# Spreading a norm's factors over the partitions: one full-precision product replaced by two rounded products of a high and a low part

## The chip, the cores and the metric

The kernel runs on one core of a Trainium2 chip. The metric is the device time of one execution in microseconds. TensorE (PE in the profile) does the matrix products, VectorE (DVE), ScalarE (ACT) and GpSimd (POOL) the element-wise work, and transfers are issued from SyncE's and ScalarE's queues.

## What is computed

One decoder layer over 2048 positions with 1024 channels, in float32, and a last norm. Cut to what matters:

```python
def rms_norm(x, g):
    y = x * lax.rsqrt(jnp.mean(x * x, axis=-1, keepdims=True) + EPS)
    return y * g

h = rms_norm(x, norm1_g)
proj = h @ w_in                       # 1024 x 2048
a = spatial_gating(proj[..., :1024])  # gelu, layer norm, 128 x 128 mixing
c = conformer_conv(proj[..., 1024:])  # gate, causal conv of width 31, norm, silu
x = x + concat([a, c]) @ w_out
h = rms_norm(x, norm2_g)              # the "second norm"
x = x + square(relu(h @ w_ff1)) @ w_ff2
return rms_norm(x, final_g)           # the "last norm"
```

The norm's factor is one number per position: 1/sqrt(mean of squares + eps).

## The kernel before

Channels lie on the partitions and positions on the free axis. The 2048 positions are worked in four blocks of 512 (blocks 0 to 3); blocks 0 and 1 form pair 0, blocks 2 and 3 form pair 1 of the feed-forward part. All large products are made from float32 operands split into a high part (rounded to fp32r) and a low part (the rest), with three fp32r products in place of one full-precision product (`mm3`). The two feed-forward matrices are multiplied with a seven-product scheme (the numbers 1 to 7 in `ORDER`, `BANK`, `INTO`).

**Stages in order.** For each block the value and gate projections (`stage_v`, `stage_g`) with the convolution as a chain of 31 VectorE steps per channel group that runs in the background; then the output projection (`stage_o`) with the residual. Block 0's `stage_o` stands before block 3's `stage_v`, and block 1's behind block 3's `stage_g`. Then `multiply("u0")` is the first feed-forward matrix for pair 0, `stage_o` of blocks 2 and 3 follow, then `multiply("u1")`, and last sixteen `down_chunk` calls, eight per pair, for the second matrix.

**The factors.** In the second norm the squares of a block are added up on GpSimd; `feature_sums` sums them over the partitions with eight short products (tile `ssum`), so that the sum of a position lies on a partition. VectorE makes `ve` (mean and eps) and GpSimd the power -1/2 (tile `r`, 128 x 4). To multiply by the factor where positions lie on the free axis, the 512 factors must stand in every partition. `spread` (and in the last norm `times_ident`) writes the identity scaled by each of the four columns of `r` to a 128 x 512 tile `dg` on VectorE, and a product with a matrix of ones (tile `rbc`) puts each factor in all partitions. This product is made in full float32, which the trace shows as two MATMUL instructions. The second norm's result is copied by ScalarE to `r_rows`, and used by `up_out` when the first feed-forward product is taken out of its bank. The last norm's result (tile `rbc3` in the program; the profile shows it as `rbc`) is used by eight VectorE multiplications that make the output.

**Who calls it.** `row_scale(b)` is called once for each block 0 to 3 at the end of its `stage_o`. `later(n, f)` runs `f` n beats on: the sums in one beat, `rsqrt` one beat on, `spread_out` two on (it issues the `dg` multiplication), `product` three on (it issues the product), and the copy to `r_rows` four on. A beat is one group of twelve products in `stage_o` and in `multiply`. `finish(b, acc)` does the last norm of blocks 0 and 1 in steps, with the pauses `gaps` between them, while the second half of the `down_chunk` calls runs. Block 3 goes through `finish_third` and block 2 through `finish_last`; the first norm goes through `make_h` and `stage_v`.

**Order of the work.** Each engine works its instructions in the order in which they were issued to it. Blocks marked `tc.manual_schedule()` keep the program's order: `stage_o` of all blocks, both `multiply` calls and the last `down_chunk`. In the others (`stage_v`, `stage_g`, the first fifteen `down_chunk` calls) a list scheduler sets the order on each engine. A planner inside the kernel keeps a clock for each engine, with a cost per instruction (`dve`, `dsb`, `gps`, `pe`, `pe4`), and uses it for two choices: `background` issues convolution steps while VectorE's clock is more than `SLACK` behind TensorE's, and `rest` gives a low part to GpSimd or to VectorE.

Temporary tiles of 128 x 512 (`tmp`) come from a ring of ten, tiny tiles (`small`) from rings of four.

Of the kernel before, what the change touches and what calls it, by code (L numbers as in the profile page):

```python
# [9 lines left out]
F32 = mybir.dt.float32  # L10
F32R = mybir.dt.float32r
BF16 = mybir.dt.bfloat16
AF = mybir.ActivationFunctionType
ALU = mybir.AluOpType

P = 128
# [66 lines left out]
def hybrid_block_kernel(  # L83
# [15 lines left out]
    dve = Clocked(nc.vector, lambda n: 0.35 if n <= 128 else 0.17 + n / 960.0)  # L99
    dcv = Clocked(nc.vector, lambda n: 0.15 + n / 960.0, dve.clock)  # L100
    dsb = Clocked(nc.vector, lambda n: 0.22 + n / 512.0 if n <= 512 else n / 640.0, dve.clock)
    gps = Clocked(nc.gpsimd, lambda n: 0.35 + n / 488.0 if n > 8 else 1.1)
    pe = Clocked(nc.tensor, lambda n: 0.0135 + n / 2400.0)
    pe4 = Clocked(nc.tensor, lambda n: 0.0135 + n / 600.0, pe.clock)

    const = ctx.enter_context(tc.tile_pool(name="const", bufs=1))
    small = ctx.enter_context(tc.tile_pool(name="small", bufs=4))
# [32 lines left out]
    def tmp(name, dtype=F32):  # L140
        return t2.tile([P, 512], dtype, tag="tmp", name=name)
# [4 lines left out]
    def mm_tile(name):  # L146
        return bank("mm", name)

    def tp_tile(name):
        return bank("tp", name)  # L150

    def tiny(name, n=4):
        return small.tile([P, n], F32, tag=f"{name}{n}", name=name)

    def act_pair(name):
        return slot(f"{name}_hi", F32R), slot(f"{name}_lo", F32R)

    def split(src, hi, lo):

        nc.scalar.copy(hi, src)  # L160
        rest(src, hi, lo)
# [13 lines left out]
    def halves(pair):  # L175
        return [(pair[0][:, a * 512:a * 512 + 512], pair[1][:, a * 512:a * 512 + 512])
                for a in range(2)]
# [56 lines left out]
    ident = const.tile([P, P], F32, name="ident")  # L234
    make_identity(nc, ident)
    ones = const.tile([P, P], F32, name="ones")
# [11 lines left out]
    def v(off, j):  # L248
        return vec[:, off + j:off + j + 1]

    def rsqrt(dst, src, mul):
        n = dst.shape[1]
        ve = tiny("ve")
        dve.tensor_scalar(ve[:, :n], src, mul, EPS, op0=ALU.mult, op1=ALU.add)
        gps.tensor_tensor(dst, ve[:, :n], nhalf.to_broadcast([P, n]), op=ALU.pow)
# [148 lines left out]
    def norm1(b, r):  # L404

        ss = tiny("ss")
        xin = []

        def load(i):
            xin.append(slot("xin"))  # L410
            nc.sync.dma_start(xin[i], x[(4 * b + i) * P:(4 * b + i + 1) * P, :])

        load(0)
        for i in range(4):
            if i < 3:
                load(i + 1)
            yield
            junk = t2.tile([P, 1024], BF16, tag="tmp", name="junk")
            nc.scalar.activation(junk, xin[i], AF.Square, accum_out=ss[:, i:i + 1])
        rsqrt(r, ss, 1.0 / D)  # L420

    def spread(r, ps):

        dg = tmp("dg")
        n = r.shape[1]
        dsb.tensor_tensor(
            dg.rearrange("p (n t) -> p n t", t=P)[:, :n, :],
            ident.unsqueeze(1).to_broadcast([P, n, P]),
            r.unsqueeze(2).to_broadcast([P, n, P]), op=ALU.mult)
        yield  # L430
        pe4.matmul(ps, ones, dg[:, :n * P], start=True, stop=True)

    def make_h(b, h):
        r = tiny("r1")
        yield from norm1(b, r)
        yield
        ps = tp_tile("rbc")
        yield from spread(r, ps)
        hf = []

        def load(k):
            hf.append(tmp("hf"))
            nc.sync.dma_start(hf[k], xt[b, k // 2, :, k % 2, :])

        load(0)
        for k in range(KD):
            if k < KD - 1:
                load(k + 1)
            yield
            if k % 2 == 0:  # L450
                pair = halves(act_pair("h"))
            dve.scalar_tensor_tensor(
                hf[k], hf[k], v(V_G1, k), ps, op0=ALU.mult, op1=ALU.mult)
            split(hf[k], *pair[k % 2])
            h.append(pair[k % 2])
# [32 lines left out]
    def feature_sums(acc, n, pc=None):  # L488

        pc = tp_tile("ssum") if pc is None else pc  # L490
        for i in range(n):
            for k, sq in enumerate(acc):
                pe4.matmul(pc[:, i:i + 1], sq[:, i * P:(i + 1) * P], ones[:, 0:1],
                           start=k == 0, stop=k == len(acc) - 1)
        return pc[:, :n]
# [100 lines left out]
    def later(n, f, first=False):  # L596
        due.append([n, f, first])
# [25 lines left out]
    def row_scale(b):  # L623

        r = r2[b]

        def spread_out():
            ps = tp_tile("rbc")
            g = spread(r, ps)
            next(g)  # L630

            def product():
                next(g, 0)
                later(1, lambda: nc.scalar.copy(r_rows[:, b % 2, :], ps))
            later(1, product)

        def sums():
            ps = feature_sums(acc[b], 4)
            later(1, lambda: rsqrt(r, ps, 1.0 / D))
            later(2, spread_out)  # L640
        return sums
# [100 lines left out]
    queue.append(make_cbias())  # L742
    late, rows0 = stage_v(0, h[0], parts[0], r0)
    queue.append(make_h(1, h[1]))
    stage_g(0, h[0], parts[0], late, rows0)
    drain()
    late, _ = stage_v(1, h[1], parts[1])
    queue.append(make_h(2, h[2]))
    slow.append(first_units())
    stage_g(1, h[1], parts[1], late)  # L750
    drain()
    late, _ = stage_v(2, h[2], parts[2])
    queue.append(split_mix(parts[0], mix[0]))
    queue.append(load_resids(0))
    stage_g(2, h[2], parts[2], late)
    drain()
    queue.append(make_h(3, h[3]))
    dve.time += BEHIND
    with tc.manual_schedule():
        stage_o(0, lambda d: tick(1))  # L760
    drain()
    late, _ = stage_v(3, h[3], parts[3])
# [212 lines left out]
    def up_out(pair):  # L975
        kept = {}

        def out(m, i, ps):
            blk_ = INTO[i]
            def copy():  # L980
                kept[m, blk_] = tmp("c")
                nc.scalar.copy(kept[m, blk_], ps)  # L982

            def finish():
                if i == 4:
                    src, c = ps, tmp("c")
                else:
                    c = kept.pop((m, blk_))
                    src = c if i == 7 else ps
                    dve.tensor_tensor(src, ps, c, op=ALU.add)  # L990
                (dsb if i == 7 else dve).scalar_tensor_tensor(
                    c, src, 0.0, r_rows[:, blk_[1], :], op0=ALU.max, op1=ALU.mult)
                later(1, lambda: nc.scalar.activation(c, c, AF.Square))  # L993
                later(2, lambda: nc.scalar.dma_start(
                    f_d[pair][m // 2, 2 * blk_[0] + blk_[1], :, m % 2, :], c))

            later(1, copy if i in (1, 5, 6) else finish, True)
        return out
# [65 lines left out]
    with tc.manual_schedule():  # L1064
        stage_o(2, at_o2)
        pace["w2"] = 0.0
        k = w2st.at[2]
# [58 lines left out]
    def finish(b, acc):  # L1126

        gaps = (6, 3, 4)
        for _ in range(gaps[0]):
            yield  # L1130
        r = tiny("r1")
        ve = tiny("ve")
        ps = feature_sums(acc, 4, mm_tile("ssum"))
        yield
        dve.tensor_scalar(ve, ps, 1.0 / D, EPS, op0=ALU.mult, op1=ALU.add)
        gps.tensor_tensor(r, ve, nhalf.to_broadcast([P, 4]), op=ALU.pow)
        for _ in range(gaps[1]):
            yield
        dg = tmp("dg")
        times_ident(dg, r)  # L1140
        for _ in range(gaps[2]):
            yield
        ps = mm_tile("rbc3")
        pe4.matmul(ps, ones, dg, start=True, stop=True)
        x = dn["x"][b]
        for k in range(KD):
            yield
            dve.scalar_tensor_tensor(x[k], x[k], v(V_FG, k), ps, op0=ALU.mult, op1=ALU.mult)
            nc.sync.dma_start(out[b, k // 2, :, k % 2, :], x[k])

    def times_ident(dg, r):
        dsb.tensor_tensor(
            dg.rearrange("p (n t) -> p n t", t=P), ident.unsqueeze(1).to_broadcast([P, 4, P]),
            r.unsqueeze(2).to_broadcast([P, 4, P]), op=ALU.mult)
# [235 lines left out]
```

## Time and profile before

| | us |
|---|---|
| three runs | 1828.97, 1831.97, 1837.33 |
| median | 1831.97 |
| profiled execution, its time | 1831.89 |
| profiled execution, its span | 1830.2 |

The span runs from the first to the last instruction of the core; 1.7 us of the execution lie around it. A row of the profile gives the engine, the operation, the tile written and the tiles read, the shape and the count, and then the busy time or the duration. L78 is the line of the helper that records nearly every operation, so rows are told apart by their tiles. A row of the timeline begins with the start and the duration in us; in brackets at its end stands how long the engine sat idle before it, and what ended that.

### The profile page before, as it was taken

How to read it: one execution, taken by the hardware profiler on the slowest of the kernel's cores; microseconds unless marked ns; L12 is line 12 of the kernel's file. 1: busy time of each engine (PE TensorE's matmuls, PEld its weight loads, DVE VectorE, ACT ScalarE, POOL GpSimd, SP SyncE). 2: the span in 40 equal slices, each digit the busy share in tenths (PEclk: the TensorE clock that was granted, in tenths of full speed). 3: DMA queues.
4: the chain of work that ended last, by engine and by line, in shares of the span. 5: the costliest groups of instructions: out<-in, count | busy, mean ns of one | idle time of the engine just before them, and what ended most of it. 6: DMA issues, size and time to landing. Idle time of an engine off the chain costs nothing. (4 is left out here: it accounts for less than half of the span.)

```text
span 1830.2 us, 23249 instructions
## 1 busy us (share of the span) xinstructions
PE 1809.3 (99%) x8080; PEld 1488.5 (81%) x8080; DVE 1330.8 (73%) x1825; ACT 758.6 (41%) x1172; POOL 1233.3 (67%) x775
## 2 busy tenths in 40 slices
PE   9999999999999999999999999999999999999998
PEld 6888878888888888888888888888788888888886
DVE  5699997997998985632567787676866568665655
ACT  6345565454445445455354545432322231212112
POOL 4575975883766666699878989776945465444434
PEclk9999999999999999999999999999999999999999
DMA  8342655432645456685557778998987679767652
GB/s 327 112 164 91 229 178 213 184 125 83 220 150 189 161 195 202 215 293 204 208 184 266 270 258 298 355 408 335 412 326 248 252 272 327 299 238 256 254 191 93
DMA packets 131686, 424.74 MB, mean 232 GB/s; under 512 B 14576, under 2 KB 15216, under 8 KB 131568
## 3 DMA queue, kind: packets, MB, share of 16 engines
q1 hardware_dynamic: 96000, 329.12, 50.5%
q10 hardware_dynamic: 35568, 94.13, 13.2%
q8 instruction: 64, 1.05, 0.2%
q14 instruction: 54, 0.44, 0.1%
HBM read 302.60 MB, written 120.59 MB: 231 GB/s over the span
## 5 line engine op out<-in xcount | busy, mean ns | idle before, releaser
L78 PE MATMUL py<-fo_hi,w2o 128*128 128x512 f32 x1792 | 555.9, 391 | 0.8 <-DVE x L78 0.8
L78 POOL TENSOR_TENSOR fo_lo<-fraw,fo_hi 128x1024 fp32r<-128x1024 f32 x111 | 274.4, 2481 | 252.9 <-ACT fo_hi L160 210.7
L78 DVE TENSOR_TENSOR x<-py,x 128x512 f32<-128x512 f32 x448 | 300.9, 687 | 185.8 <-PE py L78 185.4
L78 PEld LDWEIGHTS py<-fo_hi,w2o 128*128 128x128 f32 x1792 | 337.1, 188 | 72.0 <-DVE x L78 1.2
L78 PE MATMUL py<-hop,w1o 128*128 128x512 f32 x1536 | 363.8, 390 | 0.5 <-ACT c L982 0.4
L78 PE MATMUL py<-fo_lo,w2o 128*128 128x512 f32 x896 | 349.7, 390 | 0.9 <-POOL fo_lo L78 0.8
L78 PEld LDWEIGHTS py<-hop,w1o 128*128 128x128 f32 x1536 | 287.6, 188 | 62.4 <-issue 1.4
L78 DVE SCALAR_TENSOR_TENSOR acc<-g,vec,acc 128x512 f32<-128x512 f32 x464 | 322.9, 746 | 1.2
L160 ACT CAST fo_hi<-fraw 128x1024 fp32r<-128x1024 f32 x112 | 117.0, 1052 | 413.7 <-PE py L78 218.0
L78 POOL TENSOR_TENSOR w_lo<-raw,w_hi 128x1024 fp32r<-128x1024 f32 (+1 forms) x94 | 224.1, 2392 | 53.9 <-ACT w_hi L160 39.6
L78 POOL TENSOR_TENSOR w1o<-wraw,w1o 128x512 fp32r<-128x512 f32 x120 | 172.0, 1438 | 55.6 <-ACT w1o L810 43.4
L78 PEld LDWEIGHTS py<-fo_lo,w2o 128*128 128x128 f32 x896 | 168.6, 188 | 37.9 <-POOL fo_lo L78 2.6
L78 PE MATMUL pz<-hop,w1o 128*128 128x512 f32 x768 | 183.8, 390 | 0.0
L78 POOL TENSOR_TENSOR w1o<-ws,w1o 128x512 fp32r<-128x512 f32 x90 | 128.7, 1433 | 66.4 <-ACT w1o L810 62.6
L78 PEld LDWEIGHTS pz<-hop,w1o 128*128 128x128 f32 x768 | 143.8, 188 | 29.8
L78 DVE TENSOR_TENSOR fraw<-fraw 128x1024 f32<-128x1024 f32 x64 | 93.1, 1455 | 13.3 <-POOL fo_lo L78 13.2
L993 ACT ACTIVATE c<-c 128x512 f32<-128x512 f32 x128 | 80.8, 631 | 52.5 <-DVE c L78 52.0
L78 PE MATMUL po<-m_hi,w_hi 128*128 128x512 f32 x256 | 101.1, 395 | 0.0
L78 PE MATMUL po<-m_hi,w_lo 128*128 128x512 f32 x256 | 99.8, 390 | 0.6 <-POOL w_lo L78 0.6
L78 PE MATMUL po<-m_lo,w_hi 128*128 128x512 f32 x256 | 99.7, 389 | 0.0
L78 DVE TENSOR_TENSOR px<-px,c 128x512 f32<-128x512 f32 x32 | 22.3, 698 | 100.9 <-PE px L78 67.8
L78 POOL TENSOR_TENSOR w2p<-wraw,w2p 128x512 fp32r<-128x512 f32 x64 | 93.5, 1463 | 2.6 <-ACT w2p L810 2.6
(155 smaller groups left out, 2947.9 us busy)
## 6 DMA issues: line engine op xcount, KB each, us to landing
w2o<-w_d SPq DMA_DIRECT2D x224, 512.0 KB, 6.0
w_d<-w2p ACTq DMA_DIRECT2D x112, 512.0 KB, 5.4
wraw<-in_w SPq DMA_DIRECT2D x92, 512.0 KB, 4.7
f_d<-c ACTq DMA_DIRECT2D x128, 256.0 KB, 4.1
fraw<-f_d SPq DMA_DIRECT2D x64, 512.0 KB, 6.8
raw<-in_w_ct SPq DMA_DIRECT2D x48, 512.0 KB, 5.0
raw<-in_w_o SPq DMA_DIRECT2D x32, 512.0 KB, 5.4
w1o<-w_d SPq DMA_DIRECT2D x28, 512.0 KB, 5.5
```

What stands on the lines that cost most here:

```text
L78: return op(out, *args, **kwargs)
L160: nc.scalar.copy(hi, src)
L993: later(1, lambda: nc.scalar.activation(c, c, AF.Square))
```

## The change

Two new functions are added, and two callers use them. `r_pair` copies `r` to a tile rounded to fp32r (`rh`), subtracts to get the rest (`rl`), and makes two scaled identities. `r_sum` makes two fp32r products into one bank, the high part and then the low part.

```diff
+    def r_pair(r):
+        n = r.shape[1]
+        rh, rl = [small.tile([P, n], F32R, tag=f"rh{n}", name="rh") for _ in range(2)]
+        dve.tensor_copy(rh, r)
+        dve.tensor_tensor(rl, r, rh.bitcast(F32), op=ALU.subtract)
+        pair = [tmp("dg", F32R) for _ in range(2)]
+        for dg, part in zip(pair, (rh, rl)):
+            dsb.tensor_tensor(
+                dg.rearrange("p (n t) -> p n t", t=P)[:, :n, :],
+                ident.unsqueeze(1).to_broadcast([P, n, P]),
+                part.bitcast(F32).unsqueeze(2).to_broadcast([P, n, P]), op=ALU.mult)
+        return pair
+
+    def r_sum(ps, pair):
+        for k, dg in enumerate(pair):
+            pe.matmul(ps, ones.bitcast(F32R), dg, start=k == 0, stop=k == 1)
...
         def spread_out():
             ps = tp_tile("rbc")
-            g = spread(r, ps)
-            next(g)
+            pair = r_pair(r)
             def product():
-                next(g, 0)
+                r_sum(ps, pair)
                 later(1, lambda: nc.scalar.copy(r_rows[:, b % 2, :], ps))
...
-        dg = tmp("dg")
-        times_ident(dg, r)
+        pair = r_pair(r)
         for _ in range(gaps[2]):
             yield
         ps = mm_tile("rbc3")
-        pe4.matmul(ps, ones, dg, start=True, stop=True)
+        r_sum(ps, pair)
```

The second hunk is in `row_scale` (blocks 0 to 3), the third in `finish` (last norm, blocks 0 and 1). The other spreads keep the full-precision product.

## The prediction

> **What bounds the kernel now.** I read the page's busy times first, then the chain of work that ended last, then the waits of TensorE, and last the timeline of VectorE, GpSimd and TensorE around each of the six spreads that change.
>
> ```profile
> span 1830.2 us, 23249 instructions
> PE 1809.3 (99%) x8080; PEld 1488.5 (81%) x8080; DVE 1330.8 (73%) x1825; ACT 758.6 (41%) x1172; POOL 1233.3 (67%) x775
> ```
>
> TensorE is busy for 1809.3 of 1830.2 us. So any TensorE time that is taken away is gained, and any wait that TensorE gets is lost, wherever it happens. The chain shows what a product costs in the row of products, and so what the change can win:
>
> ```profile
> 1513.68 0.86 PE rbc L78 x2
> 1514.54 18.60 PE py L78 x82
> ...
> 1544.97 0.86 PE rbc L78 x2
> ```
>
> An fp32r product of 128x512 moves the chain on by 18.60/82 = 0.227 us. A full-precision spread (two MATMULs) moves it on by 0.86. Today TensorE hardly ever waits for the scaled identity; this is the only such row among its waits (sum, count, longest):
>
> ```profile
> PE rbc L78 <- DVE dg L78: 0.3, 1, 0.3
> ```
>
> **The gain on TensorE.** Each of the six spreads loses one product of 0.86 and gets two of 0.227: 0.86 - 0.454 = 0.41 us less. Six of them are 2.5 us, 0.14% of the time. That is all there is to win.
>
> **The price on VectorE.** Before the product VectorE does one 128x512 multiplication (`dg`). After the change it does four operations in a row: a copy of 128x4, a subtraction of 128x4 and two multiplications. TensorE takes its instructions in order, so if the second multiplication isn't done when TensorE gets to the second product, everything behind it waits. How long the four take hangs on GpSimd. Block 1 shows it (VectorE's row, then GpSimd's, then TensorE's):
>
> ```profile
> 501.35 1.79 DVE L78 TENSOR_TENSOR dg<-ident,r 128x512 f32<-128x512 f32 x1 [1.13 <-POOL r L78]
> ```
> ```profile
> 501.29 1.30 POOL L78 TENSOR_TENSOR hop<-xr,hop 128x512 fp32r<-128x512 f32 x1
> 502.55 1.75 POOL L78 TENSOR_TENSOR hop<-xr,hop 128x512 fp32r<-128x512 f32 x1
> ...
> 501.29 7.99 POOL L78 TENSOR_TENSOR hop<-xr,hop 128x512 fp32r<-128x512 f32 x6
> ```
> ```profile
> 505.22 1.02 PE L78 MATMUL rbc<-dg,ones 128*128 128x512 f32 x2
> ```
>
> GpSimd begins its next work 0.06 us before `dg` can start. `dg` ends 0.6 us after the GpSimd instruction's successor starts (503.14 against 502.55), and that successor takes 1.75 in place of 1.30. So the two don't run together: VectorE waits for the end of one GpSimd instruction, takes 0.6, and holds up the next one by 0.46. Undisturbed, these six follow each other by (7.99 - 0.46)/6 = 1.26.
>
> The copy and the subtraction are not in the trace. Their nearest rows are other 128x4 operations from on-chip memory to on-chip memory, such as `nb`. Three cases of it, and GpSimd beside the longest:
>
> ```profile
> L78 DVE SCALAR_TENSOR_TENSOR nb<-mv,rs x16: 150/846/5953, 133.7 to 694.3; 128x4 f32<-128x4 f32 x16
> ```
> ```profile
> 385.13 0.15 DVE L78 SCALAR_TENSOR_TENSOR nb<-mv,rs 128x4 f32<-128x4 f32 x1
> ...
> 478.71 1.24 DVE L78 SCALAR_TENSOR_TENSOR nb<-mv,rs 128x4 f32<-128x4 f32 x1 [0.91 <-POOL rs L78]
> 342.25 5.95 DVE L78 SCALAR_TENSOR_TENSOR nb<-mv,rs 128x4 f32<-128x4 f32 x1 [1.77 <-POOL rs L78]
> ```
> ```profile
> 478.65 1.29 POOL L78 TENSOR_TENSOR hop<-xr,hop 128x512 fp32r<-128x512 f32 x1
> ...
> 342.18 2.40 POOL L78 TENSOR_TENSOR w_lo<-raw,w_hi 128x1024 fp32r<-128x1024 f32 x1
> 344.53 1.30 POOL L78 TENSOR_TENSOR sq<-sq 128x512 f32<-128x512 f32 x1
> 345.78 2.40 POOL L78 TENSOR_TENSOR w_lo<-raw,w_hi 128x1024 fp32r<-128x1024 f32 x1
> ```
>
> At 478.71 `nb` ended with the GpSimd instruction that was running (479.94). At 342.25 it ended only with the third in a row (348.18). At 385.13 nothing stood in its way, and it took 0.15. So a tiny operation costs between 0.15 and 5.95. I take one GpSimd instruction each, as in the middle case, because it is the nearest in place (the same `hop` work, the same 1.29), and keep both ends for the range.
>
> The Trainium skill, "SBUF — State Buffer", section "Who interferes with whom", says that a VectorE copy in its two-port mode, or an operation with two on-chip inputs, shares a port pair with GpSimd under an exclusive lock, and that the later one blocks until the first finishes. By that rule each of the four new operations waits for one GpSimd instruction, which gives the forecast below; the row of 342.25, which waited for three, goes beyond it and gives the slower rival.
>
> **Site by site.** Block 1, from the rows above: the copy is let in at 502.55, the subtraction at 503.81, the first multiplication at 505.07, done 505.67; GpSimd is then held to 506.79 (505.07 + 1.26 + 0.46), the second multiplication is done at 507.39. The second product ends 0.23 later, at 507.62. Before, the spread ended at 505.22 + 0.86 = 506.08. So the end comes 1.5 us later, the 0.41 included.
>
> Block 3 has the same picture (dg to product 3.86 us, as against 3.87, and six `hop` in a row):
>
> ```profile
> 902.45 1.79 DVE L78 TENSOR_TENSOR dg<-ident,r 128x512 f32<-128x512 f32 x1 [1.13 <-POOL r L78]
> ```
> ```profile
> 902.38 8.89 POOL L78 TENSOR_TENSOR hop<-xr,hop 128x512 fp32r<-128x512 f32 x6
> ```
> ```profile
> 906.31 1.02 PE L78 MATMUL rbc<-dg,ones 128*128 128x512 f32 x2
> ```
>
> Again +1.5. Block 2 has more room (6.8 us):
>
> ```profile
> 854.13 2.90 DVE L78 TENSOR_TENSOR dg<-ident,r 128x512 f32<-128x512 f32 x1 [0.53 <-POOL r L78]
> ```
> ```profile
> 854.07 2.41 POOL L78 TENSOR_TENSOR w_lo<-raw,w_hi 128x1024 fp32r<-128x1024 f32 x1
> 856.43 2.98 POOL L78 TENSOR_TENSOR hop<-xr,hop 128x512 fp32r<-128x512 f32 x2
> ```
> ```profile
> 860.97 1.02 PE L78 MATMUL rbc<-dg,ones 128*128 128x512 f32 x2
> ```
>
> Copy 856.43, subtraction 857.69, first multiplication from 858.95, GpSimd's next one held to 860.67, second done 861.27, product done 861.50, against 861.83 before: -0.3.
>
> The last norm of block 0 (its product is the chain's row at 1513.68, ended 1514.54):
>
> ```profile
> 1508.43 1.13 DVE L78 TENSOR_TENSOR dg<-ident,r 128x512 f32<-128x512 f32 x1
> ```
> ```profile
> 1507.73 4.34 POOL L78 TENSOR_TENSOR sq<-sq 128x512 f32<-128x512 f32 x3
> 1512.04 2.38 POOL L78 TENSOR_TENSOR fo_lo<-fraw,fo_hi 128x1024 fp32r<-128x1024 f32 x1
> ```
>
> Undisturbed the three end at about 1509.0, 1510.3 and 1511.6: copy, subtraction, first multiplication. Then the `fo_lo` holds VectorE up for 2.38 + 0.46, to 1514.4; the second multiplication is done at 1515.0 and the product at 1515.3: +0.7. Here a list scheduler sets the order, so this is the roughest of the terms: -0.41 if it finds a better order.
>
> The last norm of block 1 and block 0 of the second norm have room:
>
> ```profile
> 1537.81 2.29 DVE L78 TENSOR_TENSOR dg<-ident,r 128x512 f32<-128x512 f32 x1
> 383.88 0.68 DVE L78 TENSOR_TENSOR dg<-ident,r 128x512 f32<-128x512 f32 x1
> ```
> ```profile
> 1541.61 2.40 POOL L78 TENSOR_TENSOR fo_lo<-fraw,fo_hi 128x1024 fp32r<-128x1024 f32 x1 [2.06 <-ACT fo_hi L160]
> 385.15 2.41 POOL L78 TENSOR_TENSOR w_lo<-raw,w_hi 128x1024 fp32r<-128x1024 f32 x1 [1.42 <-ACT w_hi L160]
> ```
>
> In the first, GpSimd is idle from 1539.55 to 1541.61; the copy goes then, and the other three (0.15 + 0.68 + 0.68) are done by 1541.2, with the product at 1544.97. In the second, the last multiplication is done by 388.2 even if it waits for the `w_lo`, and the product stands after block 3's projection, at 391.9. Each keeps its -0.41.
>
> **What else moves.** Behind the four operations VectorE's queue holds convolution steps, residual combinations and bank evictions. They come later by up to the stall; TensorE comes later by the same, so I cost them at nothing. If that cover fails, a bank is freed late and TensorE waits once more, by about an eviction (0.69). The kernel's own clocks shift too: VectorE is charged 1.92 us more per spread (two times 0.35 and one more 1.22), TensorE 0.41 less. So two or three convolution steps are issued a beat later, hidden as before. ScalarE's copy to `r_rows` stands a beat behind the product and follows it. No transfer is moved past a queue.
>
> **The sum.** -0.41 (block 0) + 1.5 (block 1) - 0.3 (block 2) + 1.5 (block 3) + 0.7 and -0.41 (last norm) = +2.6 us. The profiled execution took 1831.89, 0.08 from the median of the runs, so I add it there: 1834.5.
>
> **The rivals.**
>
> *The tiny operations slip in free.* If copy and subtraction take 0.15 each, block 1's first multiplication is done at 503.15, GpSimd held to 504.27, the second done at 504.9, before TensorE asks for it (505.45). Likewise at the other sites, and only the gain is left: -2.5, 1829.4. For it speaks the row at 385.13; against it that `r` comes from GpSimd, so that GpSimd has just gone on to its next instruction whenever the copy starts (the two rows at 501.29 and 501.35).
>
> *They starve behind a run of GpSimd work* (the slower side). In blocks 1 and 3 six `hop` stand in a row. If a tiny operation misses the gaps, as at 342.25, it goes when the run ends, 501.29 + 6 x 1.26 = 508.85; the multiplications follow and the product ends at about 510.5: +4.4, and the same in block 3. In block 2 two missed gaps put the product's end at 864.0: +2.2; in the last norm of block 0 they give +3.3. With -0.82 for the two easy sites the sum is +13.5: 1845.4. More than 0.5% (9.2 us) needs starving at three of the four sites. For it: 5.95 us is in the trace. Against it: the median `nb` took 0.846.
>
> *The change doesn't do what it says.* If the bitcast ones made TensorE run full-precision products, each spread would hold two of 0.86: 1.27 more than two fp32r products, six times, 7.6 on top of the forecast, 1842.1. Against it: every split product here is fp32r and takes 0.227.
>
> **How the numbers follow.** The forecast has 0.50, the free case 0.30, starving at most sites 0.15 (slower by over 0.5% in 0.09 of it), full-precision products 0.02 and an unforeseen order in the scheduled part 0.03. The range goes from the free case, less 1.4 for the spread of runs (1828.97 to 1837.33 before), to starving in two sites (2.6 + 2 x 2.9 = 8.4, so 1840.3) and 1.7 more: 1828.0 to 1842.0. About 0.5% is what a measurement of this kernel can tell from no change. Faster by that needs 9.2 us, and the whole gain is 2.5: 0.02. Slower 0.11, the same 0.87.
>
> **What would show it.** Right: twelve fp32r products on `rbc` that each move TensorE on by 0.227; TensorE waits on `dg` of one to two us near 505 and 906, none near 391 and 1545; copy and subtraction of about 1.2 us each near 501 and 902. Wrong: no such waits (the free case), copies of several us (starving), or TensorE waits elsewhere.

## The result and the profile after

The change makes the kernel slower by a little: 1837.28 us median (1833.52 to 1844.23, 15 runs) against 1831.97 (1828.97 to 1837.33, 15 runs), a ratio of 1.0032 with a 95% interval of 1.0018 to 1.0045. That is 5.3 us by the medians and 5.9 by the ratio, whose interval leaves 3.3 to 8.2. The forecast was 1834.5, no change that can be told; what came is clear of the noise and stays under the 0.5% (9.2 us) that the prediction asked for.

The execution that was profiled is the longest of the fifteen (1844.23). Its page begins:

```profile
span 1842.5 us, 23260 instructions
PE 1813.0 (98%) x8080; PEld 1492.2 (81%) x8080; DVE 1358.8 (74%) x1844; ACT 760.4 (41%) x1172; POOL 1238.9 (67%) x774
```

VectorE has 19 instructions more (18 of the change, and one low part that moved over from GpSimd) and 28 us of busy time. Products that both kernels have show where TensorE falls behind. The sums of squares of blocks 0, 1 and 3, those of the last norm of block 1, and the first spread of block 3's last norm stand in the timeline before at these times:

```profile
367.08 0.95 PE L78 MATMUL ssum<-ones,sq 128*128 128x1 f32 x8
...
496.11 0.94 PE L78 MATMUL ssum<-ones,sq 128*128 128x1 f32 x8
...
897.20 0.95 PE L78 MATMUL ssum<-ones,sq 128*128 128x1 f32 x8
...
1532.98 0.95 PE L78 MATMUL ssum<-ones,sq 128*128 128x1 f32 x8
...
1812.73 1.02 PE L78 MATMUL rbc<-dg,ones 128*128 128x512 f32 x2
```

and after at these:

```profile
372.78 0.95 PE L78 MATMUL ssum<-ones,sq 128*128 128x1 f32 x8
...
503.18 0.94 PE L78 MATMUL ssum<-ones,sq 128*128 128x1 f32 x8
...
903.80 0.94 PE L78 MATMUL ssum<-ones,sq 128*128 128x1 f32 x8
...
1538.07 0.95 PE L78 MATMUL ssum<-ones,sq 128*128 128x1 f32 x8
...
1824.03 1.02 PE L78 MATMUL rbc<-dg,ones 128*128 128x512 f32 x2
```

TensorE is late by 5.7, 7.1, 6.6, 5.1 and 11.3 us. The first 5.7 us arise ahead of the first changed instruction, so they aren't the change's (the two groups of runs, further down, have their cause). From there on 1.4 us are added by 503, hardly anything in blocks 1 to 3, 1.5 us are won back in the last norm of block 0 (where the clock had fallen in the profile before), and 6.2 us are added around the last norm of block 1. TensorE's waits after (sum, count, longest):

```profile
PE ct L78 <- ACT c L304: 4.2, 1, 4.2
PE rbc L78 <- DVE dg L78: 3.5, 3, 1.8
PE sgu L78 <- ACT gv L603: 3.0, 1, 3.0
PE py L78 <- DVE x L78: 2.0, 2, 1.3
...
PE ct L78 <- DVE c L78: 1.5, 1, 1.5
```

The wait for the scaled identity has grown from 0.3 to 3.5 us, in three places. VectorE's four operations in block 1, GpSimd's work beside them, and TensorE's two products there:

```profile
508.94 1.25 DVE L78 CAST rh<-r 128x4 fp32r<-128x4 f32 x1 [1.13 <-POOL r L78]
510.22 1.21 DVE L78 TENSOR_TENSOR rh<-r,rh 128x4 fp32r<-128x4 f32 x1
511.36 2.37 DVE L78 TENSOR_TENSOR dg<-ident,rh 128x512 fp32r<-128x512 f32 x2
```
```profile
508.88 7.25 POOL L78 TENSOR_TENSOR hop<-xr,hop 128x512 fp32r<-128x512 f32 x5
```
```profile
512.29 0.39 PE L78 MATMUL rbc<-dg,ones 128*128 128x512 f32 x1
513.78 0.50 PE L78 MATMUL rbc<-dg,ones 128*128 128x512 f32 x1 [1.10 <-DVE dg L78]
```

Copy and subtraction take one GpSimd instruction each, 1.25 and 1.21 us for 128x4 numbers, and TensorE waits 1.10 us for the second part. In block 3 the same rows give a wait of 0.59. In block 2 TensorE doesn't wait.

The last norm of block 1 was to be an easy site. After, VectorE's rows there are:

```profile
1542.79 0.68 DVE L78 TENSOR_TENSOR x<-py,x 128x512 f32<-128x512 f32 x1
1544.00 2.35 DVE L78 CAST rh<-r 128x4 fp32r<-128x4 f32 x1 [0.53 <-POOL r L78]
1546.39 2.31 DVE L78 TENSOR_TENSOR rh<-r,rh 128x4 fp32r<-128x4 f32 x1
1548.62 3.46 DVE L78 TENSOR_TENSOR dg<-ident,rh 128x512 fp32r<-128x512 f32 x2
1552.01 0.68 DVE L78 TENSOR_TENSOR x<-py,x 128x512 f32<-128x512 f32 x1
1552.61 2.80 DVE L78 TENSOR_TENSOR fraw<-fraw 128x1024 f32<-128x1024 f32 x1
1555.33 3.67 DVE L78 TENSOR_TENSOR x<-py,x 128x512 f32<-128x512 f32 x6
```
```profile
1543.94 10.39 POOL L78 TENSOR_TENSOR fo_lo<-fraw,fo_hi 128x1024 fp32r<-128x1024 f32 x4
```

The list scheduler has put the copy right behind `r`. GpSimd has just gone on to long low parts (`fo_lo`, 2.4 us, four in a row), and copy and subtraction wait for one each. For 8 us no bank is evicted (`x<-py,x` at 1542.79 and then at 1552.01), and the eviction after that, at 1555.33, stands behind a sum (`fraw`) that takes 2.80 us in place of its usual 1.22. TensorE, and its granted clock in the windows of 5 us (start and end, length, busy time, clock, share of DMA, GB/s):

```profile
1549.91 0.39 PE L78 MATMUL rbc<-dg,ones 128*128 128x512 f32 x1
1552.14 0.50 PE L78 MATMUL rbc<-dg,ones 128*128 128x512 f32 x1 [1.84 <-DVE dg L78]
1556.06 0.79 PE L78 MATMUL py<-fo_hi,w2o 128*128 128x512 f32 x1 [1.28 <-DVE x L78]
```
```profile
1545.00:1550.00 5.00, 5.00 (x24) 1.00 0.49 172
1550.00:1555.00 5.00, 2.79 (x9) 0.89 0.99 363
1555.00:1560.00 5.00, 3.94 (x9) 0.50 0.36 148
1560.00:1565.00 5.00, 5.00 (x22) 0.93 0.92 328
```

TensorE waits 1.84 us for the identity, then 1.28 us for the eviction at 1555.33, and the granted clock falls. It is 0.50 in the whole third window, in which 3.94 us of products do the work of 1.97.

### The profile page after: what moved, and what is told of

Its sections match the earlier page's. It is cut to its first block, busy times and chain, and to the rows that moved or that the text cites. A ratio compares the mean times of both kernels' runs of the same rounds, so it can differ in the third digit from the quotient of the medians.

```text
span 1842.5 us, 23260 instructions
## 1 busy us (share of the span) xinstructions
PE 1813.0 (98%) x8080; PEld 1492.2 (81%) x8080; DVE 1358.8 (74%) x1844; ACT 760.4 (41%) x1172; POOL 1238.9 (67%) x774
```

## The experiments

The theory is that the loss is lateness: the four VectorE operations queue behind GpSimd, and TensorE waits for them. The rival is that the change gives a worse order elsewhere (the planner's clocks shift, and so does the list scheduler's order).

**The halves.** `row_scale` alone (the second hunk of the change) and `finish` alone (the third).

```diff
 # rows only: finish as before
-        pair = r_pair(r)
+        dg = tmp("dg")
+        times_ident(dg, r)
...
 # last norm only: row_scale as before
-            pair = r_pair(r)
+            g = spread(r, ps)
+            next(g)
...
```

> The change in row_scale alone (four sites), the last norm as before. Late-identity theory (TensorE waits for the second scaled identity because VectorE's four operations each queue behind GpSimd): by the trace after, blocks 1 and 3 cost 0.9 and 0.4 us net, blocks 0 and 2 gain 0.41 each, so about +0.5 us, 1.000; the rest of the +5.3 is the last norm. Rival, changed order (the planner's clocks and the list scheduler give a worse order in the stages behind): it moves more instructions than the other half, so it should carry most of the loss, +3 to +5 us, 1.002 to 1.003.

> The change in finish alone (last norm of blocks 0 and 1), the second norm as before. Late-identity theory: nearly the whole loss, +3 to +6 us, with TensorE waiting about 2 us for the scaled identity of block 1's last norm, a wait for an eviction behind it, and a stretch of granted clock near 0.5. Rival, changed order: little, 0 to +2 us.

Measured: rows only 1.0023 (1.0007 to 1.0039), last norm only 1.0012 (0.9996 to 1.0029). By the ratios they add up to the whole, but the shares (+4.2 and +2.2 us) came out nearer to the rival's. In the trace of the rows TensorE waits 1.7 us for `dg`, as the theory has it, and 1.5 us at a new place, which the traces of the whole change and of the next experiment have too, and those of the last norm alone and of the kernel before have not. In the whole change it is this row:

```profile
477.66 0.66 PE L78 MATMUL ct<-ident,c 128*128 128x128 f32 x4 [1.55 <-DVE c L78]
```

A transposition waits for the last step of a convolution chain. Before, VectorE made that step 16.8 us behind the first residual of block 1's output projection (462.72 and 445.88); now it is 25.7 us behind it (476.87 and 451.21), with 4.34 us of idling for a GpSimd `hop` queued ahead of it. So the rival holds for 1.5 us: the order did get worse in one place. 1.7 + 1.5 - 4 x 0.41 is +1.6, not +4.2; the rest is taken up below. In the last norm alone TensorE's wait is not for `dg` but 2.1 us for the eviction behind it, and its clock stays at 1.00.

**More time.** The products are issued one beat later in `row_scale`, and two steps later in `finish`.

```diff
-                later(1, lambda: nc.scalar.copy(r_rows[:, b % 2, :], ps))
-            later(1, product)
+                nc.scalar.copy(r_rows[:, b % 2, :], ps)
+            later(2, product)
-        gaps = (6, 3, 4)
+        gaps = (6, 3, 6)
```

> The whole change, with the products issued later: one beat in row_scale (the copy to r_rows stays in its beat) and two steps more in finish. Late-identity theory: the waits on dg go, only the gain of 0.41 us each is left, -2.5 us against before, 0.9985 to 1.000. Rival, changed order: the order is as far from the order before as with the change, so still +3 to +6 us.

Measured: 0.9986 (0.9971 to 1.0001), 1829.79 us median. In block 1 VectorE's four operations take as long as with the change (1.26, 1.21 and 2.38), but no wait on `dg` is left among TensorE's. The convolution's 1.5 us are still there. The lost time is back; a gain of 2.5 us fits the ratio, though its interval just reaches no change. The rival had this at +3 to +6. In the last norm of block 1 the experiment isn't clean: the order changed there too, and copy and subtraction took 0.17 and 1.56 us in place of 2.35 and 2.31.

**The tiny operations on GpSimd.** GpSimd makes `r`, and now `rh` and `rl` behind it.

```diff
-        dve.tensor_copy(rh, r)
-        dve.tensor_tensor(rl, r, rh.bitcast(F32), op=ALU.subtract)
+        gps.tensor_copy(rh, r)
+        gps.tensor_tensor(rl, r, rh.bitcast(F32), op=ALU.subtract)
```

> The whole change, with the copy and the subtraction on GpSimd, right behind the power that makes r; VectorE keeps the two multiplications. Late-identity theory: the two tiny operations no longer queue behind other GpSimd work, VectorE's part is shorter by 1.2 to 4 us at each site, TensorE's waits on dg shrink to under 0.5 us each, time -2 to 0 us against before. Rival, changed order: still +3 to +6 us.

Measured: 0.9988 (0.9973 to 1.0004), 1830.77 us. GpSimd's rows in block 1, and TensorE's wait in the whole kernel:

```profile
499.37 1.30 POOL L78 TENSOR_TENSOR hop<-xr,hop 128x512 fp32r<-128x512 f32 x1
500.61 0.19 POOL L78 CAST rh<-r 128x4 fp32r<-128x4 f32 x1
500.88 0.70 POOL L78 TENSOR_TENSOR rh<-r,rh 128x4 fp32r<-128x4 f32 x1
```
```profile
PE rbc L78 <- DVE dg L78: 0.6, 2, 0.4
```

What took VectorE 1.25 and 1.21 us takes 0.19 and 0.70 in GpSimd's own row, and the wait falls from 3.5 to 0.6 us. This trace hasn't the convolution's wait either, so the run takes both causes away at once; TensorE's waits for a low part (`fo_lo`) are 2.2 us in place of 0.8.

**One operation more, and two fewer.** The first adds a tiny copy in front; the second leaves out the low part (so the factors are rounded to fp32r).

```diff
 # one more
+        dve.tensor_copy(rl.bitcast(F32), r)
-        dve.tensor_copy(rh, r)
+        dve.tensor_copy(rh, rl.bitcast(F32))
 # high part only
         dve.tensor_copy(rh, r)
-        dve.tensor_tensor(rl, r, rh.bitcast(F32), op=ALU.subtract)
-        pair = [tmp("dg", F32R) for _ in range(2)]
+        pair = [tmp("dg", F32R)]
...
```

> The whole change with one more tiny operation at each site: r is first copied as it is, and the copy is then rounded. Nothing else is added. Late-identity theory: each tiny operation that queues behind GpSimd puts the second scaled identity off by about 1.2 us more, which TensorE waits out in blocks 1 and 3 and in the last norm and partly in block 2, so +3 to +6 us on top of the change, 1.0045 to 1.007 against before. Rival, changed order: the order hardly moves, 1.003 as with the change.

> The low part is left out: one copy, one multiplication and one fp32r product at each of the six sites, so the factors are rounded. Late-identity theory: with two operations in place of four nothing is late (block 1: 1.25 + 0.6 to 1.8 us of 3.9), and the product gains 0.86 - 0.227 = 0.63 us, six times: -3.8 us, 0.998. Rival, changed order: +2 to +6 us as with the change.

Measured with one more: 1.0042 (1.0026 to 1.0058), median 1840.82. That is a tenth of a per cent over the change by the ratios and 3.5 us by the medians, though the two were measured apart; the time lies at the theory's lower edge and its interval reaches down to the rival's value, so the time alone doesn't settle it. The trace does: the wait grows from 3.5 to 7.9 us, in six places at four of the six sites: two in block 1, one in block 2, two in block 3 and one in the last norm of block 1. The convolution's wait isn't in it.

```profile
PE rbc L78 <- DVE dg L78: 7.9, 6, 1.9
```

With the high part only: 0.998 (0.9965 to 0.9994), 1829.05 us; the -3.8 us of six times 0.63 lie well inside that interval. The one wait on `dg` left among TensorE's (0.3 us) is at a spread that wasn't changed, and the kernel before has it too.

**The two groups of runs.** The runs of the kernel before fall into two groups: of the 35 beside the first experiments, 19 lie from 1829.5 to 1833.0 and 16 from 1834.3 to 1840.2. In the profile after, the 4.2 us wait (`ct <- ACT c`) stands in a part that is the same in both kernels. VectorE, GpSimd and TensorE there:

```profile
270.54 6.71 DVE L78 SCALAR_TENSOR_TENSOR nb<-mv,rs 128x4 f32<-128x4 f32 x1
```
```profile
269.87 2.41 POOL L78 TENSOR_TENSOR w_lo<-raw,w_hi 128x1024 fp32r<-128x1024 f32 x1
272.21 0.22 POOL L549 COPY halo<-g 128x30 f32<-128x30 f32 x1
272.37 2.53 POOL L78 TENSOR_TENSOR m_lo<-part,m_hi 128x512 fp32r<-128x512 f32 x2
274.83 2.36 POOL L78 TENSOR_TENSOR w_lo<-raw,w_hi 128x1024 fp32r<-128x1024 f32 x1
277.12 0.23 POOL L545 COPY g<-halo 128x30 f32<-128x30 f32 x1
```
```profile
278.86 1.11 PE L78 MATMUL ct<-ident,c 128*128 128x128 f32 x4 [4.21 <-ACT c L304]
```

A 128x4 operation waits until a whole run of GpSimd work has passed, ScalarE's `c` waits for it, and TensorE for `c`. In the profile before, the same instruction took 1.81 us at 269.95; in both it started 0.67 us behind the same `w_lo`. Behind the wait the granted clock is 0.50 from 278 to 284, and TensorE is 6.8 us late, of which 5.7 are left at 372.78. The profiles of rows alone (1839.0) and of the later products (1835.01) have this wait too (3.7 and 3.9 us), those of the kernel before (1831.89), of the last norm alone (1833.9) and of the tiny operations on GpSimd (1828.86) don't. But the profile with one operation more (1845.28) hasn't it either, so it isn't all that makes a run long. To test it, `nb` was made on GpSimd, in the kernel before and in the change with `rh` and `rl` on GpSimd:

```diff
-        dve.scalar_tensor_tensor(nb, mv[:, :, 0], -1.0, rs, op0=ALU.mult, op1=ALU.mult)
+        gps.tensor_tensor(nb, mv[:, :, 0], rs, op=ALU.mult)
+        gps.tensor_tensor(nb, nb, minus.to_broadcast([P, 4]), op=ALU.mult)
...
```

(`minus` is a constant of -1; the same stands in both places that make `nb`.)

> The kernel before, with the 128x4 shift nb of the layer norms made by two GpSimd multiplications in place of one VectorE operation; the spreads are untouched. Theory of the two groups of runs (a tiny VectorE operation is passed over while GpSimd's instructions follow each other, for 6.7 us at nb in the profile after, and TensorE runs dry): the group of longer runs goes, the median falls by 1 to 4 us, 0.998 to 0.9995, and the runs lie within 4 us. Rival, the groups have another cause: both groups stay and the ratio is 1.000 or, with GpSimd's added work, above.

> The whole change with copy and subtraction on GpSimd, and nb on GpSimd as well. If both theories hold the gains add: -2 us from the products and -1 to -4 us from nb, 0.997 to 0.9985 against before, one group of runs. If only the first holds, 0.9988 and two groups.

Measured: `nb` alone 0.9983 (0.9969 to 0.9997), both 0.9952 (0.9934 to 0.9971), 1825.25 us median. The second beats both kernels, by more than was expected (0.997 to 0.9985); its six runs lie within 4 us (1823.78 to 1827.58). With `nb` alone the runs still spread over 6.6 us (1828.41 to 1834.99), not within 4 as expected. In its profile (1833.21) `ve`, another 128x4 operation that stayed on VectorE, took 9.70 us, and TensorE waited 2.3 us behind it.

**The halves once more.** With `nb` on GpSimd as the ground, the ground again, and on it the whole change and each half.

> The kernel before with nb on GpSimd, once more, as the ground for the three runs beside it, which have the same nb. 0.9983 of before, as it gave already; both theories say the same.

> The whole change on that ground. Late-identity theory: as much slower than the ground as the change is than the kernel before, +4 to +6 us, with fewer long runs. Rival, the loss comes from nb waiting longer or oftener after the change: it goes with nb, and only the gain is left, -2.5 us against the ground.

> The change in row_scale alone on that ground. If the +4.2 us of that half were its own waits: +3 to +5 against the ground. If they were mostly longer nb waits in nine of its twelve runs (its waits on the identity were 1.1 and 0.6 us in the trace, less four gains of 0.41): 0 to +1.

> The change in the last norm alone on that ground. If the last norm carries most of the loss (its four VectorE operations hold up evictions and TensorE's clock falls after the wait): +2.5 to +4 against the ground. If the halves are alike: +2.

| against the kernel before | ratio | 95% interval | median us |
|---|---|---|---|
| ground | 0.9980 | 0.9965 to 0.9994 | 1829.54 |
| whole change on it | 1.0000 | 0.9985 to 1.0014 | 1832.01 |
| rows on it | 0.9976 | 0.9959 to 0.9992 | 1829.35 |
| last norm on it | 0.9997 | 0.9982 to 1.0011 | 1831.34 |

On this ground the change costs 2.5 us by the medians and 3.7 by the ratios, the rows nothing (-0.2 and -0.7), and the last norm 1.8 and 3.1. Each ratio is known to about 2.6 us to each side, so for the whole the rival's -2.5 is out, and the first theory's +4 is not. For the rows the "0 to +1" is nearer than the "+3 to +5"; for the last norm the runs can't choose.

The traces on this ground show the lateness again, smaller. With the whole change TensorE waits 0.61, 0.61 and 0.34 us for `dg` and 1.81 us for the eviction, at a clock of 1.00: less the gain of 2.5 that is +0.9. With the rows it waits 0.62 and 0.60, less four gains: -0.4. With the last norm it waits 0.20 and 1.96, less two gains: +1.3. The convolution's 1.5 us are in none of them. The ground and the last norm on it have a wait of 1.0 us at another convolution step (`cb`), and the rows and the whole change haven't: here the changed order wins.

The long runs aren't gone: the profiled run of the last norm on this ground took 1837.66, and there `ve` was held up once more:

```profile
332.56 9.71 DVE L78 TENSOR_SCALAR ve<-mv 128x4 f32<-128x4 f32 x1
```

## Why the prediction was right or wrong

- **The gain on TensorE** was right. Where nothing is late, the whole change comes out at 0.9986 against the 2.5 us predicted (0.14%), and one product fewer at 0.998 (predicted 3.8 us, 0.2%). The intervals are 2.7 us to each side, so the times fit the gain and don't measure it.
- **One GpSimd instruction for each tiny operation** was right in the second norm's blocks 1 to 3: 1.25 and 1.21 us in block 1, 1.26 and 1.21 in block 3. In block 0 nothing stood in their way (0.14 and 0.16).
- **Blocks 1 and 3** were right in kind and too dear: waits of 1.10 and 0.59, so about +0.7 and +0.2 with the gain in, not +1.5 each. The term was mis-sized by one step. The first multiplication follows the subtraction at once; it doesn't wait for another GpSimd instruction (of the eight `dg` of rows alone the median is 0.68 us and the longest 1.78). The four took 508.94 to 513.73, which is 4.8 us, not the 6.0 that I had from 501.35 to 507.39.
- **Block 2 and block 0** were right: no wait.
- **The last norm of block 0** was wrong in sign (+0.7); the way out that the prediction named, -0.41 with a better order, is what came. The list scheduler placed other products between the two, which start 0.69 us apart, and TensorE doesn't wait there.
- **The last norm of block 1** is the step that failed: "In the first, GpSimd is idle from 1539.55 to 1541.61; the copy goes then". I took the place of the old multiplication for the place of the copy. In the scheduled part the copy was moved up to directly behind `r`, where GpSimd had just started something, and GpSimd's idle stretch wasn't there: four `fo_lo` follow each other from 1543.94 to 1554.33. It costs 3.1 us of waits and about 2.6 us of clock (half of 3.94 us, and the two windows beside it at 0.89 and 0.93), in place of -0.41.
- **"TensorE comes later by the same, so I cost them at nothing"** failed twice. There an eviction queued behind the four, and behind a sum that GpSimd held up, was late by 1.28 us more than TensorE was; the prediction's own price for such a failure was 0.69. And the convolution steps that were to be "hidden as before" gave a wait of 1.55 us at 477.66.
- **The rival of starving** was right as a mechanism but in the wrong place. No copy or subtraction was passed over in any of these traces; the longest took 2.39 us, one long GpSimd instruction. The old `nb` and `ve` were, in both kernels.

The sum behind the first changed instruction: +1.5 (convolution), +4.7 (the weight loads in front of the three late products waited 1.44, 1.03 and 2.27 us, a little more than the products' own idle time of 3.5), +1.3 (eviction), +2.6 (clock), -2.5 (gain), and -1.6 for a clock fall ahead of block 0's last norm that only the profile before has (last section), so +6.0 in all; the trace shows 12.3 - 5.7 = 6.6. The median's +5.3 is of that size, and the forecast of +2.6 was short by the last norm of block 1 and the convolution. That it came so near is partly luck: blocks 1 and 3 and the last norm of block 0 were about 3 us too dear together, the last norm of block 1 about 6 too cheap, and the convolution's 1.5 weren't in it. What stays open is the share of chance: rows alone gave +4.2 with only +1.6 in the trace, nine of its twelve runs are of the longer group, and on the ground with `nb` on GpSimd they cost nothing. Whether the change makes `nb` wait oftener, or the runs fell so, these runs don't tell.

## What to carry to other kernels

A cheaper product pays only if what feeds it stays in time: count the instructions on the way to it, not their sizes. A 128x4 VectorE operation issued right behind a GpSimd result costs a whole GpSimd instruction at most sites here (1.2 to 2.4 us), so put such crumbs on the engine that makes their input, or issue the consumer a beat later; the two turned +5.3 us into -1.6 and -2.5 by the medians, with intervals that just reach no change. Where a list scheduler sets the order, don't take an old instruction's place for that of its replacement.

## What the runs showed of the hardware

- **A tiny VectorE operation can be passed over.** No 128x512 multiplication `dg` took over 2.90 us in any of these traces, which is one long GpSimd instruction (2.4 us) and little more, but 128x4 operations took up to 5.95, 6.71, 9.71 and 10.45 us (`nb` before, `nb` after, `ve` with the last norm on the ground, `nb` with the high part only), through several GpSimd instructions that followed each other. The Trainium skill, "SBUF — State Buffer", section "Who interferes with whom", has the later one blocked until the first finishes; the measurement goes beyond that. What decides whether an operation is passed over these runs don't show: the same `nb`, started 0.67 us behind the same `w_lo`, took 1.81 us in one run and 6.71 in another.
- **A short wait can halve TensorE's clock, or not.** The same wait of 1.0 us for `sq` ahead of the last norm's sums was followed by a clock of 0.70 in the profile before (first line) and of 1.00 in the profile after (second line):

```profile
1502.00:1506.00 4.00, 3.71 (x15) 0.70 0.79 300
```
```profile
1509.00:1513.00 4.00, 3.65 (x20) 1.00 0.81 296
```

After the wait of 1.84 us in the last norm of block 1 the clock was at 0.50 before the wait of 1.28 us (from 1554.78) had begun. A wait of 2.13 us at the same place in the last norm alone left it at 1.00:

```profile
1553.00:1554.00 1.00, 1.00 (x5) 0.93 0.99 393
1554.00:1555.00 1.00, 0.78 (x2) 0.50 1.04 426
```
```profile
1546.00:1549.00 3.00, 1.18 (x5) 1.00 0.75 307
1549.00:1552.00 3.00, 3.00 (x15) 1.00 0.00 0
```

The Trainium skill, "TensorE: Matmul & The Clock Gate", section "Part 1: The HAM clock gate (the "warmup" mystery)", says that half rate follows an idle window of about 3.4 us and that the windows run freely. Here waits of 1.0 and of 1.84 us were enough, each well under that; that like waits come out differently in different runs fits windows that run freely, but these runs don't test it.
